# Two transformer-like layers on one core: ten more gate tiles by seven products, the residual stream in DRAM, normalized rows in whole tiles

## The chip, the core and the metric

The kernel runs on one NeuronCore of one Trainium2 chip. The metric is the device time of one execution in microseconds (us). Three executions of the kernel before took 2176.94, 2178.32 and 2180.31 us; the median is 2178.32 us. Times in this document that are stamped like 571.04 are microseconds from the start of the profiled span.

## What is computed

Two layers, each with three sublayers around a residual stream x of 512 tokens by 1024 features. Every sublayer normalizes x, does its work, normalizes the result and adds it to x. In outline, from the reference:

```python
for l in range(DEPTH):                                   # DEPTH = 2
    h = rms_norm(x, gn[0])
    x = x + 0.5 * rms_norm(swiglu(h, w_ffn1_gate[l], w_ffn1_up[l], w_ffn1_down[l]), gn[1])
    h = rms_norm(x, gn[2])
    proj = h @ w_in[l]
    hq, hf, hi, hg, aq, ak, av, gate_a, gate_b = jnp.split(proj, IN_SPLITS, axis=-1)
    y_hg = hgrn2_mixer(hq, hf, hi, hg, lb_all[l], hgrn_head_gain[l]) @ w_branch_hgrn[l]
    y_at = swa_sink_attention(aq, ak, av, attn_sinks[l]) @ w_branch_attn[l]
    mixed = jax.nn.sigmoid(gate_a) * y_hg + jax.nn.sigmoid(gate_b) * y_at
    x = x + rms_norm(mixed @ w_out[l], gn[3])
    h = rms_norm(x, gn[4])
    x = x + 0.5 * rms_norm(swiglu(h, w_ffn2_gate[l], w_ffn2_up[l], w_ffn2_down[l]), gn[5])
```

A swiglu is `(silu(h @ w_gate) * (h @ w_up)) @ w_down` with 2816 hidden features. gate_a and gate_b are 1024 features each: the *branch gates*, 8 tiles of 128 features each, 16 in all per layer.

## The kernel before

**Numbers in two parts.** All large products are in float32 accuracy from fp32r parts: every operand is split into hi (a cast) and lo (the rest), and one block product is three matmuls, hi by hi, hi by lo and lo by hi (mm3, L277 to L279, all recorded at L103). Weights come as tiles of 128 rows by 1024 columns into w32 (4 buffers, loads at L187 on SP's queue). ScalarE (ACT) casts them to whi (L219); wlo comes from VectorE (DVE, L226) or, for kinds v, a and d, from an ACT negation (L223) and an accumulating DMA that GpSimd (POOL) issues (L224). TensorE (PE) holds a 128x128 weight block and streams 512 tokens past it.

**Seven products for eight.** Where a gate tile and an up tile (or any two tiles of 128 features) stand over the same h, the pair is a 2x2 block product, and *fast* computes it with seven products for eight on halves: 256 tokens and half of the contraction. It needs sums of the weights (tt tiles, DVE L206, L207, L212, L213, from the two w32 tiles of the pair; items b and c of the weight stream) and sums of h (tiles x56 and x37, made by *sums* and *quarter_sums*, L340 to L348, one call per two of the eight row tiles of h, and split by L294 on ACT and L295 on DVE), and puts the products together on DVE (L682, L684, L689, L690). In the first FFN 16 of the 22 pairs go that way, in each of the other three 18: 70 in all. The first pairs of each FFN go by plain products (*quad*, *project*, *twice*), which gives DVE time to make the sums.

**The mixer** first makes the projections of the attention and of the recurrence. Then come the branch gates: *branch* makes one tile of gate by *project* (24 matmuls of 512 columns), takes a tanh (ACT L1020), multiplies the attention's or the recurrence's output by a branch weight (12 matmuls) and joins them with one DVE instruction (L1025). Eight calls are for gate_b, eight for gate_a. Beside the gate_b tiles runs the rest of the recurrence, one head after the other, as coroutines that the program steps at points set by a planner's cost table (WAIT): its matmuls stand between those of the gates in the order of PE, which is written out by hand. One step of it: the products p1 and p2 of two blocks of tokens (L828 to L841), their copies from PSUM on ACT as s1 (L835) and s2 (L842), and then, for the same head, the ten products of po (L878; PE L103 aux<-s,s 128x128), of which the fourth already reads s2; then the head's normalization (ACT L881, L884; DVE L883 to L892).

**Residual stream.** x lies in one SBUF tile, x_all, of 128 partitions by 4 by 1024. *lay* fills it at the start of the first FFN: 32 transposes on PE through three PSUM buffers (aux), copied out by ACT and DVE in turn (L401). *post* adds to it in place (L570), *norm* reads it.

**Rows of h.** For the FFNs other than the first, class Halves keeps h in halves of 256 tokens, for the mixer class Pre keeps whole rows of 512.

**Order.** PE's order is fixed by the program. ACT, DVE, POOL and the DMA queues get their instructions in an order that a scheduler settles before the run; `pin` (keep_in_program_order) ties those that are marked to the order of the program among each other. On each engine the instructions then run strictly in that order.

## Time and profile before

| | before |
|---|---|
| the three executions (median) | 2176.94, 2178.32, 2180.31 (2178.32) us |
| the profiled execution: its time, its span | 2179.35 us, 2177.6 us |
| PE busy, DVE busy, ACT busy, POOL busy (share of the span) | 99%, 63%, 48%, 6% |
| mean clock granted to TensorE | 0.998 of full |
| moved by DMA | 262.55 MB, 121 GB/s |

The span runs from the first to the last instruction; 1.75 us of the profiled time lie around it. "PE <- DVE" in a list of waits is idle time of PE that ended when DVE's result came. A row of a timeline gives the start, the duration, engine, line, operation, output and inputs, and in brackets the idle time of the engine ahead of it. Matmuls are pipelined: the duration of one is its latency, and the spacing of the starts tells the rate.

### The profile page before, as it was taken

What the parts mean: (1) busy time and instruction counts of PE and PEld (TensorE: products, weight loads), DVE (VectorE), ACT (ScalarE), POOL (GpSimd) and SP (SyncE); (2) the same over time, 40 slices, a digit from 0 to 9 for tenths busy, and PEclk for the clock granted to TensorE, in tenths of its full rate; (3) what the DMA queues carried; (4) which work ended last, traced back from release to release, by engine and by line L of the source; (5) the groups of instructions that cost most, each with busy time, mean ns of one, the idle gap of its engine ahead of it and who ended that gap; (6) DMA issues with size and microseconds to landing.
All of it is one profiled execution on the core that took longest, in us unless ns stands there. A gap on an engine that the chain in (4) does not pass through costs nothing.

```text
span 2177.6 us, 34576 instructions
## 1 busy us (share of the span) xinstructions
PE 2161.6 (99%) x13625; PEld 1951.4 (90%) x13625; DVE 1369.7 (63%) x2381; ACT 1043.5 (48%) x1703; POOL 124.2 (6%) x148
## 2 busy tenths in 40 slices
PE   9999999999999999999999999999999999999998
PEld 7999988888888999998899998898788889999987
DVE  6887725856734768783487786267566438687823
ACT  6565515354423555562355554254543336565612
POOL 0111000000000011100001110000000000111000
PEclk9999999999999999999999999999999999999999
DMA  7587632211223258773237874322112332578721
GB/s 236 121 185 180 173 97 78 87 59 59 70 95 97 81 130 182 180 203 97 73 107 162 192 184 147 96 86 68 53 64 78 97 97 88 137 179 184 187 89 39
DMA packets 126131, 262.55 MB, mean 121 GB/s; under 512 B 13360, under 2 KB 71184, under 8 KB 125968
## 3 DMA queue, kind: packets, MB, share of 16 engines
q1 hardware_dynamic: 105088, 203.13, 29.7%
q0 software_dynamic: 20736, 57.16, 15.0%
q8 instruction: 107, 1.75, 0.3%
q14 instruction: 56, 0.46, 0.1%
q10 hardware_dynamic: 144, 0.05, 0.0%
HBM read 200.99 MB, written 2.15 MB: 93 GB/s over the span
## 4 chain that ended last, share of the span: by engine, by line
PE 95%; DVE 2%; DMA 1%; ACT 1%; issue 1%; SPq 0%; POOL 0%; DVEq 0%; POOLq 0%; ACTq 0%
PE acc L103 70%; PE aux L103 23%; PE aux L110 1%; DMA w<-wall 1%; PE acc L110 1%; DMA s<-xin 0%; DVE s L453 0%; DMA wlo<-w 0%; DVE s L940 0%; DVE wlo L226 0%; DVE s L771 0%; DMA g_sb<-gains 0%; DVE s L566 0%; ACT s L509 0%; DVE s L576 0%
## 5 line engine op out<-in xcount | busy, mean ns | idle before, releaser
L103 PE MATMUL acc<-s,whi 128*128 128x256 f32 (+1 forms) x5104 | 1096.1, 312 | 1.6 <-ACT whi L219 0.9
L103 PEld LDWEIGHTS acc<-s,whi 128*128 128x128 f32 x5104 | 833.2, 191 | 48.3 <-DVE s L701 1.1
L103 PE MATMUL acc<-s,wlo 128*128 128x256 f32 (+1 forms) x2552 | 791.0, 310 | 0.1
L219 ACT CAST whi<-w 128x1024 fp32r<-128x1024 f32 (+1 forms) x373 | 360.7, 969 | 664.0 <-PE aux L103 270.0
L226 DVE TENSOR_TENSOR wlo<-w,whi 128x1024 fp32r<-128x1024 f32 (+1 forms) x229 | 278.5, 1218 | 405.1 <-ACT whi L219 399.6
L103 PEld LDWEIGHTS acc<-s,wlo 128*128 128x128 f32 x2552 | 487.2, 191 | 26.2 <-DVE wlo L226 0.4
L103 PE MATMUL acc<-whi,s 128*128 128x512 f32 x1296 | 425.2, 393 | 0.0
L103 PEld LDWEIGHTS acc<-whi,s 128*128 128x128 f32 x1296 | 243.9, 188 | 51.3
L103 PE MATMUL acc<-wlo,s 128*128 128x512 f32 x648 | 252.9, 390 | 0.0
L224 POOL DMA_DIRECT2D wlo<-w x144 | 124.0, 861 | 1909.9 <-DVE s L347 689.0
L103 PE MATMUL aux<-whi,s 128*128 128x512 f32 x624 | 207.8, 390 | 0.0
L103 PE MATMUL aux<-s,whi 128*128 128x256 f32 x1120 | 204.6, 283 | 0.0
L226 DVE TENSOR_TENSOR wlo<-tt,whi 128x1024 fp32r<-128x1024 f32 x140 | 170.6, 1218 | 10.1 <-ACT whi L219 9.7
L103 PEld LDWEIGHTS aux<-s,whi 128*128 128x128 f32 x1120 | 174.7, 192 | 0.0
L219 ACT CAST whi<-tt 128x1024 fp32r<-128x1024 f32 x140 | 145.7, 1041 | 26.8 <-PE acc L103 26.3
L103 PE MATMUL aux<-s,wlo 128*128 128x256 f32 x560 | 158.5, 283 | 0.0
L103 PEld LDWEIGHTS acc<-wlo,s 128*128 128x128 f32 x648 | 122.1, 188 | 23.7
L103 PEld LDWEIGHTS aux<-whi,s 128*128 128x128 f32 x624 | 117.1, 188 | 24.1
L206 DVE TENSOR_TENSOR tt<-w,w 128x512 f32<-128x512 f32 x70 | 48.4, 691 | 126.8 <-DMA w<-wall 116.9
L223 ACT ACTIVATE wlo<-w 128x1024 fp32r<-128x1024 f32 (+1 forms) x144 | 122.0, 847 | 0.0
L103 PE MATMUL aux<-wlo,s 128*128 128x512 f32 x312 | 121.4, 389 | 0.0
L103 PEld LDWEIGHTS aux<-s,wlo 128*128 128x128 f32 x560 | 107.5, 192 | 0.0
(164 smaller groups left out, 1888.2 us busy)
## 6 DMA issues: line engine op xcount, KB each, us to landing
w<-wall SPq DMA_DIRECT2D x283, 512.0 KB, 3.5
w<-wall SPq DMA_DIRECT2D x352, 128.0 KB, 2.6
wlo<-w POOLq DMA_DIRECT2D x74, 512.0 KB, 6.0
wlo<-w POOLq DMA_DIRECT2D x70, 256.0 KB, 4.1
grow<-rows_d SPq DMA_DIRECT2D x6, 512.0 KB, 4.9
s<-xin SPq DMA_DIRECT2D x8, 256.0 KB, 6.7
y<-s SPq DMA_DIRECT2D x8, 256.0 KB, 2.5
w<-wall SPq DMA_DIRECT2D x2, 256.0 KB, 4.1
```

Of the source, the lines that this page charges most:

```text
L103: nc.tensor.matmul(o, lhsT, rhs, start=start, stop=stop)
L110: nc.tensor.transpose(o, src, ident)
L206: nc.vector.tensor_tensor(self.t13[:, h[0]], w[:, h[0]], v[:, h[0]], op=ALU.add)
L219: i = nc.scalar.copy(it.hi[:, c], w[:, c])
L223: nc.scalar.mul(it.lo[:, c], w[:, c], -1.0)
L224: nc.gpsimd.dma_start(it.lo[:, c].bitcast(F32), w[:, c], accum_op=ALU.add)
L226: nc.vector.tensor_tensor(it.lo[:, c], w[:, c], it.hi[:, c].bitcast(F32), op=ALU.subtract)
```

## The change

Four things at once.

1. **Branch gates.** Of the 16 tiles per layer, six (the first six of gate_b, `LATE = 6`) stay as they were. The last two of gate_b and the eight of gate_a go in pairs through `sevenths`, the body of the old *fast*: five pairs per layer, seven products for eight, 84 matmuls of 256 columns for 48 of 512. The tanh reads the joined result m (for the second tile of a pair with scale -0.5). The weight stream gets the matching items (`gates`).
2. **Sums one tile ahead.** `sums` now belongs to Pre. In the mixer it is called four times, before the gate_b tiles 2, 3, 4 and 5; in an FFN other than the first twice before the first gates and once before each of the next two. Each call makes, from whole rows, two additions of 512 columns (L450), the four quarter sums (L352 to L355, 256 columns each) and two splits of 512 columns (ACT L302, DVE L303).
3. **Whole rows of h.** Halves goes; the FFNs use Pre. The two plain pairs that went by *twice* (two passes of 256 columns) go by *project* (512 columns).
4. **Residual in DRAM.** x_all goes; 48 pieces of 128x512 are stored to x_d after `lay` (L411) and after each `post` (L558), and loaded again late in each `down` (L523). The pool of large tiles grows from 53 to 61.

Besides, three DVE instructions are now pinned: the first weight sum of each pair (before L206, now L214) and the gating multiplications (before L701 and L707, now L682 and L688). The core of the diff:

```diff
-SLOTS = 53
+SLOTS = 61
-W32, WS, AHEAD, TAIL, PLAIN, FIRST, EARLY = 4, 6, 3, 2, 4, 6, 4
+W32, WS, AHEAD, TAIL, PLAIN, FIRST, EARLY, LATE = 4, 6, 3, 2, 4, 6, 4, 6
...
-    x_all = const([P, TT, D], "x_all")
-    xt = [[x_all[:, t, h * S : (h + 1) * S] for h in range(2)] for t in range(TT)]
+    x_d = dr.tile([TT, 2, P, S], F32, name="x_d")
...
-                nc.vector.tensor_tensor(self.t13[:, h[0]], w[:, h[0]], v[:, h[0]], op=ALU.add)
+                pin(nc.vector.tensor_tensor(self.t13[:, h[0]], w[:, h[0]], v[:, h[0]], op=ALU.add))
...
-                    (nc.vector.tensor_copy if h else nc.scalar.copy)(xt[t][h], p)
+                    x = big()
+                    (nc.vector.tensor_copy if h else nc.scalar.copy)(x, p)
+                    nc.sync.dma_start(x_d[t, h], x)
...
+        def sums(self):
+            k = len(self.x56)
+            a = []
+            for hi, lo in (self.h[k], self.h[k + 4]):
+                f = big()
+                nc.vector.tensor_tensor(f, hi.bitcast(F32), lo.bitcast(F32), op=ALU.add)
+                a.append([f[:, c] for c in HALF])
+            for x, v in zip((self.x56, self.x37), quarter_sums(a[0][0], a[1][0], a[0][1], a[1][1])):
+                x.append(v)
...
         for j in range(kt // 2 - TAIL):
+            if j == kt // 2 - TAIL - 1:
+                for t in range(TT):
+                    for h in range(2):
+                        xt[t][h] = big()
+                        nc.sync.dma_start(xt[t][h], x_d[t, h])
...
                 nc.vector.scalar_tensor_tensor(xt[t][h], yg[h], rc, xt[t][h], op0=ALU.mult, op1=ALU.add)
+                if pre:
+                    nc.sync.dma_start(x_d[t, h], xt[t][h])
...
-                nc.vector.tensor_tensor(z, og, pre.rb, op=ALU.mult)
+                pin(nc.vector.tensor_tensor(z, og, pre.rb, op=ALU.mult))
...
-                if j < 4:
-                    pre.sums()
-                gated(twice(pre), twice(pre))
+                pre.sums()
+                gated(project(pre), project(pre))
...
+        def branches(get):
+            v = sevenths(pre)
+            src = get()
+            for i in range(2):
+                g = big(F32, [P, 2, H2])
+                nc.scalar.activation(out=g, in_=v[:, 2 * i : 2 * i + 2, :], func=AF.Tanh, scale=-0.5 if i else 0.5)
+                p = acc()
+                for k in range(4):
+                    wmm(p, ws.next(), src[k], k == 0, k == 3)
+                g = g.rearrange("p i t -> p (i t)")
+                nc.vector.scalar_tensor_tensor(g, g, 1.0, p, op0=ALU.add, op1=ALU.mult)
+                yield g
...
-        part = [branch(m, attended) for m in range(KT)]
+        part = []
+        for m in range(LATE):
+            if m >= LATE - 4:
+                pre.sums()
+            part.append(branch(attended))
+        part += [g for m in range(LATE, KT, 2) for g in branches(attended)]
         mixed = []
-        for m in range(KT):
-            g = branch(m, recurred)
-            nc.vector.tensor_tensor(g, g, part[m], op=ALU.add)
-            mixed.append(split(g, 0.5))
+        for m in range(0, KT, 2):
+            for g in branches(recurred):
+                nc.vector.tensor_tensor(g, g, part[len(mixed)], op=ALU.add)
+                mixed.append(split(g, 0.5))
```

Lines from here on, in the rows, are those of the kernel that the row belongs to; the changed kernel's lines are other numbers (L842 became L822, L835 became L815, L219 became L227, L226 became L234, L881 became L861, L1025 became L1005, L294 became L302).

**Place one: ACT in the mixer, at head 2 of the recurrence.** First ACT's order before, from the copy of head 2's s1 to the squares of its po; then the same stretch in the changed kernel.

```order
L835 COPY s_5715<-aux_5716 128x256
L219 CAST whi_5896<-w_965_5583 128x1024
L842 COPY s_5738<-aux_5739 128x512
L881 ACTIVATE s_5762<-aux_5751 128x512
L884 ACT_TABLE_LOAD
```

```order
L815 COPY s_5755<-aux_5756 128x256
L227 CAST whi_5974<-w_981_5623 128x1024
L302 CAST s_5785<-s_5779 128x512
L302 CAST s_5789<-s_5780 128x512
L822 COPY s_5797<-aux_5798 128x512
L861 ACTIVATE s_5821<-aux_5810 128x512
L864 ACT_TABLE_LOAD
```

Two casts of the first call of `sums` now stand ahead of the copy of s2 (L842, now L822). They read s_5779 and s_5780, which DVE makes in the next piece. At head 3 two casts of the second call stand ahead of its copy of s2 in the same way, and both places come again in layer 1.

**The same place on DVE.** The changed kernel's order from the end of gate_b tile 1 (L1005); before, the first row was followed at once by the 128x4 product, the wlo of the weights and the reduction (L883, now L863).

```order
L1005 SCALAR_TENSOR_TENSOR s_5726<-s_5726,acc_5728 128x512
L450 TENSOR_TENSOR s_5775<-s_3760,s_3761 128x512
L450 TENSOR_TENSOR s_5777<-s_3786,s_3787 128x512
L767 TENSOR_TENSOR s_5610<-s_5610 128x4
L234 TENSOR_TENSOR wlo_5975<-w_981_5623,whi_5974 128x1024
L352 TENSOR_TENSOR s_5779<-s_5777,s_5775 128x256
L355 TENSOR_TENSOR s_5780<-s_5775 128x256
L353 SCALAR_TENSOR_TENSOR s_5779<-s_5779,s_5775 128x256
L215 TENSOR_TENSOR tt_6071<-w_1003_5771 128x512
L354 SCALAR_TENSOR_TENSOR s_5780<-s_5779,s_5777 128x256
```

Two additions of 512 columns, a weight split of 1024, four of 256 columns and one more of 512 now stand between the end of the gate tile and the second cast on ACT.

**Place two: DVE at the start of the first FFN.** The names: L701 to L704 before, L682 to L685 now, are the multiplications of the plain gates 0 to 2; L206 and L207 before, L215 now, are weight sums for the first fast pair; L401 is a copy of `lay`. First the order before, then now, from the first gate's first multiplication.

```order
L701 TENSOR_TENSOR s_386<-acc_210,s_374 128x512
L703 TENSOR_TENSOR s_387<-acc_211,s_374 128x512
L701 TENSOR_TENSOR s_392<-acc_212,s_374 128x512
L703 TENSOR_TENSOR s_393<-acc_213,s_374 128x512
L701 TENSOR_TENSOR s_453<-acc_340,s_374 128x512
L704 TENSOR_TENSOR s_387<-s_387,s_386 128x512
L704 TENSOR_TENSOR s_393<-s_393,s_392 128x512
L1092 TENSOR_SCALAR hgh<-hgh 128x256
L1095 TENSOR_TENSOR lbmx<-lb_in 128x4
L206 TENSOR_TENSOR tt_683<-w_74_384,w_82_445 128x512
```

```order
L682 TENSOR_TENSOR s_386<-acc_210,s_374 128x512
L684 TENSOR_TENSOR s_387<-acc_211,s_374 128x512
L215 TENSOR_TENSOR tt_699<-w_82_445 128x512
L685 TENSOR_TENSOR s_387<-s_387,s_386 128x512
L682 TENSOR_TENSOR s_392<-acc_212,s_374 128x512
L684 TENSOR_TENSOR s_393<-acc_213,s_374 128x512
L685 TENSOR_TENSOR s_393<-s_393,s_392 128x512
L1093 TENSOR_SCALAR hgh<-hgh 128x256
L1096 TENSOR_TENSOR lbmx<-lb_in 128x4
```

A weight sum that reads the same load, w_82, has moved from behind the gates' multiplications to the third row. Gate 2's multiplications and the copies of `lay` on DVE stand behind all of these.

**The same place on ACT**, the changed kernel's order from gate 0's silu on. L683 is a silu, L227 and L231 are weight casts and negations, L1099 is the exp of the lower bounds, L410 a copy of `lay`. Before, the three silus stood together ahead of the exp (L702 and L1098), and behind the exp came the first copy (L401), a weight cast, two copies, a weight negation and the last copy.

```order
L683 ACTIVATE s_386<-s_386 128x512
L231 ACTIVATE wlo_573<-w_62_308 128x1024
L683 ACTIVATE s_392<-s_392 128x512
L227 CAST whi_604<-w_65_338 128x1024
L1099 ACT_TABLE_LOAD
L1099 ACTIVATE lbex<-lbex 128x8
L410 COPY s_452<-aux_447 128x512
L231 ACTIVATE wlo_605<-w_65_338 128x1024
L683 ACT_TABLE_LOAD
L683 ACTIVATE s_455<-s_455 128x512
L410 COPY s_474<-aux_469 128x512
```

The silu of gate 2 now stands behind the exp with a table load of its own, and three of ACT's four copies of `lay` stand behind it.

More of the change, by code (lines that the diff above doesn't have):

```diff
@@ L160, in pairs, with gates @@
                 self.n += 2
+        def gates(self):
+            u, h = self.n, (slice(0, D // 2), slice(D // 2, D))
+            self.src[u + 1] = [(h[0], wall[u + 1][:, h[1]]), (h[1], wall[u + 2][:, h[0]])]
+            self.src[u + 2] = [(h[0], wall[u + 1][:, h[0]]), (h[1], wall[u + 2][:, h[1]])]
+            self.pairs(1)
+            self.plain(1)
         def rows(self, kt):
@@ L421, in raw @@
         def raw(self, half, i):
-            return [x[half + i] for x in self.x124]
-    class Pre:
+            return [[x[half + i][:, j, :] for j in range(2)] for x in self.x124]
+    class Pre(Quarters):
         def __init__(self, l, n):
@@ L432, in __init__, with raw @@
             self.xn = {}
+            self.x56, self.x37 = [], []
+        def sums(self):
[7 more added lines that the diff above has]
+                x.append(v)
+        def raw(self, half, i):
+            return [cut(self.h[k + 4 * i], HALF[half]) for k in range(4)]
         def turn(self, half, get):
@@ L603, in down @@
         return pre
-    def of_half(pre, k, half):
-        h = pre.h[k]
-        if isinstance(pre, Halves):
-            return [h[half][:, i, :] for i in range(2)]
-        return h if half is None else cut(h, HALF[half])
     def quad(pre, halves):
@@ L622, in quad @@
                         blocks[k, j] = ws.next(uses=2 if halves else 1)
-                    wmm(o[j][:, c], blocks[k, j], of_half(pre, k, half), k == 0, k == KT - 1)
+                    wmm(o[j][:, c], blocks[k, j], cut(pre.h[k], c), k == 0, k == KT - 1)
             ws.pinned = False
-        return o
-    def twice(pre):
-        o = acc()
-        blocks = [ws.next(uses=2) for _ in range(KT)]
-        for half in (0, 1):
-            for k in range(KT):
-                wmm(o[:, HALF[half]], blocks[k], of_half(pre, k, half), k == 0, k == KT - 1)
         return o
@@ L1047, in trunk @@
             if n == 2:
-                ws.plain((4 * H + 4 + 2 + 2 * KT) * KT // 8 + 2 * KT * 4 // 8)
+                ws.plain(2 * H + 6 + 8 + LATE * 3 // 2)
+                for _ in range(KT - LATE // 2):
+                    ws.gates()
                 ws.rows(KT)
```

109 lines of the change are left out of this document (39 added, 70 removed).

## The prediction

> **What bounds the kernel now.** I read the page first, for the busy shares and the chain that ended last; then the list of what PE waits for; then timelines of PE, ACT and DVE where the change moves instructions.
>
> ```profile
> span 2177.6 us, 34576 instructions
> ...
> PE 2161.6 (99%) x13625; PEld 1951.4 (90%) x13625; DVE 1369.7 (63%) x2381; ACT 1043.5 (48%) x1703; POOL 124.2 (6%) x148
> ...
> PE 95%; DVE 2%; DMA 1%; ACT 1%; issue 1%; SPq 0%; POOL 0%; DVEq 0%; POOLq 0%; ACTq 0%
> ```
>
> PE is busy 99% of the span and holds 95% of the chain. So work taken from PE shortens the run by its whole length, and every wait that PE is given lengthens it by its whole length, however idle the other engines are on average.
>
> ```profile
> PE acc L110 <- DVE x_all L570: 2.5, 1, 2.5
> PE aux L103 <- DVE s L295: 1.5, 2, 0.7
> ...
> PE aux L110 <- DVE x_all L401: 0.7, 1, 0.7
> ```
>
> These are sums of PE's waits, how often, and the longest, costliest first. Apart from the end (2.5 us) no group is over 1.5. There is almost nothing to win from waits, and much room for new ones.
>
> **PE's saving.** Rates are read from the spacing of starts, not from durations. The four rows are two stretches, of 512 columns and of 256; each row is two of the three matmuls of a group.
>
> ```profile
> 627.98 0.61 PE L103 MATMUL acc<-s,whi 128*128 128x512 f32 x2
> 631.38 0.62 PE L103 MATMUL acc<-s,whi 128*128 128x512 f32 x2
> 739.97 0.40 PE L103 MATMUL acc<-s,whi 128*128 128x256 f32 x2
> 745.37 0.40 PE L103 MATMUL acc<-s,whi 128*128 128x256 f32 x2
> ```
>
> From 627.98 to 631.38 lie five groups, 15 matmuls: 3.40 / 15 = 226.7 ns each. From 739.97 to 745.37 lie 15 groups, 45 matmuls: 120.0 ns. A narrow matmul costs 6.7 ns more than half a wide one, so seven products for eight save less than an eighth.
>
> Gates: 10 pairs, each 84 x 120.0 = 10.08 us for 48 x 226.7 = 10.88: 10 x -0.80 = -8.0 us. Plain FFN pairs by whole rows: two pairs, that is four projections, in each of three FFNs, 12 x (24 x 226.7 - 48 x 120.0 ns) = 12 x -0.32 = -3.8 us. Together **-11.8 us**. TensorE: Matmul & The Clock Gate of the Trainium skill (section "Wait — 56ns, not 53.3ns?") gives columns / 2.4 GHz + 2.5 ns, that is 215.8 and 109.2 ns here, by which the two parts would be -11.9 and -0.7; this trace has neither figure (226.7 and 120.0 ns), and its rows decide.
>
> **What is added in the mixer.** The rows are ACT, PE and DVE at head 2 of the recurrence, and below them head 3.
>
> ```profile
> 570.56 0.58 ACT L842 COPY s<-aux 128x512 f32<-128x512 f32 x1 [1.16 <-PE aux L103]
> ...
> 571.04 2.39 PE L103 MATMUL aux<-s,s 128*128 128x128 f32 x20
> ...
> 569.19 0.68 DVE L1025 SCALAR_TENSOR_TENSOR s<-s,acc 128x512 f32<-128x512 f32 x1
> 569.79 0.15 DVE L787 TENSOR_TENSOR s<-s 128x4 f32<-128x4 f32 x1
> 569.86 1.21 DVE L226 TENSOR_TENSOR wlo<-w,whi 128x1024 fp32r<-128x1024 f32 x1
> ...
> 583.64 0.68 DVE L295 TENSOR_TENSOR s<-aux,s 128x512 fp32r<-128x512 f32 x1
> 584.24 0.28 DVE L833 TENSOR_SCALAR s<-s,s 128x128 f32<-128x128 f32 x1
> ...
> 586.00 0.59 ACT L842 COPY s<-aux 128x512 f32<-128x512 f32 x1 [2.13 <-PE aux L103]
> ...
> 586.50 2.17 PE L103 MATMUL aux<-s,s 128*128 128x128 f32 x18
> ```
>
> PE begins po at 571.04, and its fourth product, some 0.3 us on, reads what L842 has copied by 571.14. ACT had waited 1.16 us for that copy's input, so the copy runs as soon as it can. After the change two casts stand ahead of it, and their inputs are late. From the rows: 512 columns on DVE take 0.68 us and follow one another at 0.60 (569.19 to 569.79, 583.64 to 584.24); 256 columns and casts:
>
> ```profile
> L345 DVE SCALAR_TENSOR_TENSOR s<-s,s 128x256 f32<-128x256 f32 x16 | 6.7, 418 | 0.0
> ...
> L294 ACT CAST s<-s 128x512 fp32r<-128x512 f32 x120 | 67.6, 617 | 20.7 <-DVE s L345 19.6 <-DVE s L346 0.9
> ```
>
> With the same overlap of 0.08, 256 columns follow at 0.34. DVE from 569.79: two additions 1.20, the small product 0.07, the weight split 1.14, three quarter sums 1.02: 573.2. A weight sum 0.60 and the last quarter sum 0.42: 574.2. ACT's second cast runs from there to 574.8 and the copy to 575.4. PE wanted it at 571.36: **4.0 us** of PE idle. Nothing hides it, since PE's order is fixed and its next matmul is the one that waits.
>
> At head 3, the second call: DVE has the additions from 584.6 to 585.8 (ahead of them now stand all four small scalings, of which two came behind the split before), three quarter sums to 586.8, the last to 587.2; the casts follow from 586.9 and end by 588.0, the copy by 588.6, against 586.59 before: **2.0 us**. The third and fourth call have no PE work behind them that is due soon: 0. Both layers have the place: 2 x 6.0 = **+12.0 us**.
>
> The pairs themselves add DVE and ACT work where there is room: in the gates' stretch DVE was 17.73 us busy of 50 (first row), and in the FFNs the same body runs at 39.89 of 50 (second).
>
> ```profile
> 600.00:650.00 50.00, 17.73 (x19) 1.00 0.30 96
> 850.00:900.00 50.00, 39.89 (x57) 1.00 0.82 185
> ```
>
> **What is added at the start.** First FFN, layer 0, where `lay` copies x out of PSUM:
>
> ```profile
> 42.30 0.69 DVE L206 TENSOR_TENSOR tt<-w,w 128x512 f32<-128x512 f32 x1 [0.98 <-DMA w<-wall]
> 44.92 0.68 DVE L401 COPY x_all<-aux 128x512 f32<-128x512 f32 x1
> ...
> 41.62 1.28 ACT L1098 ACT_TABLE_LOAD   x1
> 43.71 0.59 ACT L401 COPY x_all<-aux 128x512 f32<-128x512 f32 x1 [0.34 <-PE aux L110]
> ...
> 43.08 1.93 PE L110 MATMUL aux<-ident,s 128*128 128x128 f32 x16
> 45.66 1.09 PE L110 MATMUL aux<-ident,s 128*128 128x128 f32 x8 [0.65 <-DVE x_all L401]
> 46.99 1.09 PE L110 MATMUL aux<-ident,s 128*128 128x128 f32 x8 [0.24 <-ACT x_all L401]
> 47.84 0.71 PE L103 MATMUL acc<-s,whi 128*128 128x512 f32 x2
> ```
>
> The weight sum waited for its load until 42.30, which cost nothing since the gates' multiplications were done. Now it is DVE's third row and the load is no earlier, so from 38.0 to 42.3 DVE stands, with the multiplications behind it. Then four rows of 512 bring ACT its second silu at 44.2; the cast, a table load (1.28) and the exp put ACT's first copy of `lay` at 47.3 instead of 43.71, and DVE's, behind the exp's small rows and two multiplications, at 49.3 instead of 44.92. The third copy waits for ACT's weight negation, another table load and a silu, until 50.7. PE has three buffers, so the eight groups of four transposes end at 52.6 instead of 47.84: **+4.8 us**. Where the first copy were on time, this falls to about 0.
>
> **What a wait costs beyond itself.** The last wait of PE, ahead of 2171.39, shows that the granted clock (the column after the busy times) follows idleness:
>
> ```profile
> 2168.00:2171.00 3.00, 0.94 (x5) 1.00 0.62 175
> 2171.00:2171.50 0.50, 0.11 (x1) 1.00 0.00 0
> 2171.50:2172.00 0.50, 0.50 (x4) 0.50 0.00 0
> ...
> 1.50:4.00 2.50, 2.50 (x14) 1.00 0.80 231
> 4.50:6.00 1.50, 1.50 (x15) 1.00 0.88 270
> ```
>
> After 2.45 us without work it is 0.50. How long work takes to bring it back is bounded by the start: there PE does 14 small matmuls in 2.5 us, and from about 4 us on 15 in 1.5, so nearly 3 us of work go at 1/1.78 of the rate (the column reads 1.00 there, the counts do not). That is 2.9 x (1 - 1/1.78) = 1.3 us lost. The bounds are 0 and twice that. The waits of 4.0, 4.0 and 4.8 us are all longer than 2.45; I take 1.3 for each, **+3.9 us**, and none for those of 2.0. The same page of the Trainium skill, section "What's actually happening", says that the clock is set by free-running windows of 3.4 us. The drop in this trace, 2.5 us after the last work, fits a window that was mostly idle. By that rule a wait of 4 us may fall across two windows and cool nothing, and one of 2 us could never fill one.
>
> **At nothing.** Stores and loads of x (256 KB each, SP): post's last piece of a `down` is ready, and the next weight load stands behind its store.
>
> ```profile
> 367.77 1.42 DVE L570 SCALAR_TENSOR_TENSOR x_all<-s,rt,x_all 128x512 f32<-128x512 f32 x2
> ...
> 372.54 1.46 SPq L187 DMA_DIRECT2D w<-wall  x2
> ...
> w<-wall SPq DMA_DIRECT2D x2, 256.0 KB, 4.1
> ```
>
> At 369.19 the last store can go, and the load is issued at 372.54, when its buffer comes free: 3.3 us of cover for two issues of 0.73. If the cover is gone, the gates start up to 1.5 us later in each of five places. The loads of x stand ahead of weight loads in `down`; what they wait for has no row, so 0 to one landing of their size (4.1 us) in each of six; I take 0, as the stores' row has it, and keep the rest for the upper end. The FFNs' sums keep their place beside the plain pairs (PE's 1.3 us shorter stretch there is inside their lead): 0, at worst 1.3 in each of three.
>
> **The sum.** 2179.35 - 11.8 + 12.0 + 4.8 + 3.9 = 2188.3 for a profiled run; that run lay 1.0 over the median, so **2187 us**, 0.4% slower. 0.2%, 4.4 us, is about what a measurement of this kernel can tell from no change.
>
> **Rivals.**
> - *All hidden* (the side of faster): head 2's copy decides. If DVE reached the first addition 4 us earlier than 569.79, at about 565.8, and ACT stood free at the start, only the saving would be left: 2178.3 - 11.8 = 2166.5. Against it: DVE ends the gate tile's row at 569.79, and the order puts the additions behind that row. Chance 0.12.
> - *Waits in the mixer alone*, the start hidden or the load earlier: 2178.3 - 11.8 + 12.0 + 2.6 = 2181; without cooling 2178.5. The same. Chance 0.15.
> - *Waits without cooling* (the windows of the rule fall well): 2178.3 + 5.0 = 2183.3, just slower. Chance 0.17.
> - *DVE's weight sums ahead of the joins.* In each fast pair of the FFNs the first weight sum stands now right ahead of the next pair's first join. Before, it waited 1.67 us per pair for a load:
>
> ```profile
> DVE tt L206 <- DMA w<-wall: 116.9, 50, 4.9
> ```
>
>   116.9 / 70. DVE has 10.08 - 8.0 = 2.1 us free in a pair and now also waits 0.7 for the silu. If the load comes as late as before, each pair slips by 0.3 us: 70 x 0.3 = 20, 2207 us. For it: the place. Against: that load is of a buffer that comes free a pair earlier. Chance 0.12.
>
> The forecast (2185 to 2191) has 0.44. The range leaves out most of *all hidden* and the far end of the last rival: **2174 to 2204**. Faster 0.12; same 0.16 (the second rival and the edge of the third); slower 0.72.
>
> **What would show it.** Right: PE aux L103 waits near 4 and 2 us for ACT L822 in both layers; PE L110 waits in sum near 5 us for L410; the clock at 0.5 for some 3 us behind each of the long ones; PE's rates at 226.7 and 120.0 ns. Wrong: no wait at L822 (all hidden), DVE's L215 waiting for loads in the FFNs with PE waiting behind it (the last rival), or PE waiting for whi or wlo in the branch pairs, which I have at nothing.

## The result, and the profile after

The changed kernel took 2187.57 us, the median of five executions (2184.43 to 2188.43). The kernel before took 2178.32 on the same chip (2176.76 to 2180.31). The ratio is 1.004, with a 95% interval of 1.0025 to 1.0055: slower by 0.4%, where 2187 us was predicted. The execution that was profiled is the slowest of the five, 2188.43.

The page of the changed kernel, its lines on the span, the engines, the chain that ended last, and the new stores (KB each, then median us from issue to landing):

```profile
span 2186.4 us, 35185 instructions
...
PE 2156.7 (99%) x13697; PEld 1952.8 (89%) x13697; DVE 1462.5 (67%) x2501; ACT 1104.1 (51%) x1769; POOL 141.4 (6%) x168
...
PE 94%; DVE 4%; ACT 1%; issue 0%; DVEq 0%; ACTq 0%
...
x_d<-s SPq DMA_DIRECT2D x48, 256.0 KB, 2.0
```

PE is busy 4.9 us less and the span is 8.8 us longer: PE's lead is spent on waits and, as the windows below show, on a lower clock. What PE waits for in the changed kernel (sum, times, longest):

```profile
PE aux L103 <- ACT s L822: 10.6, 4, 3.5
PE aux L110 <- ACT s L410: 3.1, 1, 3.1
PE acc L110 <- DVE s L556: 2.5, 1, 2.5
PE aux L110 <- DVE s L410: 2.0, 1, 2.0
PE aux L103 <- DVE s L303: 1.5, 2, 0.7
```

The third and fifth were there before (as L570 and L295). New are the first, the second and the fourth: the mixer's 10.6 us, and 5.1 us at the start, where the kernel before waited 0.9 (L401).

Where the two programs stand in time is read from the starts of the same matmul of PE at the ends of the stages. The last column is what each stretch alone added:

| stretch of PE, up to | before | after | added |
|---|---|---|---|
| end of the first plain gates (start of layer 0) | 50.71 | 57.11 | +6.40 |
| end of the first FFN | 372.66 | 379.06 | 0.00 |
| mixer of layer 0, up to the gate pairs | 597.27 | 609.26 | +5.59 |
| the five gate pairs | 693.25 | 701.35 | -3.89 |
| out-projection | 747.52 | 755.81 | +0.19 |
| plain pairs of the second FFN | 967.92 | 974.95 | -1.26 |
| its end | 1098.38 | 1105.60 | +0.19 |
| layer 1: plain pairs of the first FFN | 1318.77 | 1324.73 | -1.26 |
| its end | 1449.42 | 1455.39 | +0.01 |
| mixer, up to the gate pairs | 1675.69 | 1689.96 | +8.30 |
| the five gate pairs | 1771.70 | 1782.07 | -3.90 |
| out-projection | 1825.97 | 1836.54 | +0.20 |
| plain pairs of the second FFN | 2046.37 | 2055.68 | -1.26 |
| end of the span | 2177.6 | 2186.4 | -0.51 |

The sum is +8.8. The saving is -11.57, and three places give back +20.3.

**The saving.** A stretch of a gate pair on PE:

```profile
659.76 0.40 PE L103 MATMUL acc<-s,whi 128*128 128x256 f32 x2
...
664.44 0.40 PE L103 MATMUL aux<-s,whi 128*128 128x256 f32 x2
```

From 659.76 to 664.44 lie 13 groups of three: 4.68 / 39 = 120.0 ns each, the spacing that the FFNs' pairs had before. Nothing in the pairs waits.

**The mixer.** Head 2 of layer 0 on DVE:

```profile
576.21 1.28 DVE L450 TENSOR_TENSOR s<-s,s 128x512 f32<-128x512 f32 x2
577.49 1.22 DVE L234 TENSOR_TENSOR wlo<-w,whi 128x1024 fp32r<-128x1024 f32 x1
...
580.24 0.41 DVE L354 SCALAR_TENSOR_TENSOR s<-s,s 128x256 f32<-128x256 f32 x1
```

On ACT:

```profile
579.75 0.62 ACT L302 CAST s<-s 128x512 fp32r<-128x512 f32 x1 [3.92 <-DVE s L353]
580.68 0.62 ACT L302 CAST s<-s 128x512 fp32r<-128x512 f32 x1 [0.32 <-DVE s L354]
581.21 0.58 ACT L822 COPY s<-aux 128x512 f32<-128x512 f32 x1
```

On PE, here and at the same step of layer 1: the products that wait, and as the last row of each the same weight product, 28 matmuls on.

```profile
577.48 0.83 PE L103 MATMUL aux<-s,s 128*128 128x128 f32 x6
...
581.84 1.83 PE L103 MATMUL aux<-s,s 128*128 128x128 f32 x14 [3.53 <-ACT s L822]
...
586.06 0.76 PE L103 MATMUL acc<-s,whi 128*128 128x512 f32 x2
```

```profile
1659.78 3.35 PE L103 MATMUL aux<-s,s 128*128 128x128 f32 x14 [3.54 <-ACT s L822]
...
1666.76 0.53 PE L103 MATMUL acc<-s,whi 128*128 128x512 f32 x1
```

ACT stands for 3.92 us with its first cast, whose input DVE makes behind the two additions and the weight split. The copy L822 has had its input since about 577 (in E1 below, where no cast is in its way, it waits 1.16 us for it), but its place is behind both casts. PE waits 3.53 us in layer 0 and 3.54 in layer 1. The wait is the same; what follows it is not. From its end to that weight product PE takes 586.06 - 581.84 = 4.22 us in layer 0 and 1666.76 - 1659.78 = 6.98 in layer 1, for the same work. Windows of PE (busy time, granted clock, then the share and rate of DMA), cut where the clock changed and in layer 0 at the same distance, say why:

```profile
576.84:580.25 3.41, 1.47 (x10) 1.00 0.14 22
580.25:583.66 3.41, 1.82 (x15) 1.00 0.34 132
...
1655.45:1658.86 3.41, 0.79 (x7) 1.00 0.29 88
1658.87:1662.28 3.41, 2.50 (x11) 0.50 0.18 72
1662.28:1665.69 3.41, 3.41 (x11) 0.50 0.00 0
1665.70:1669.10 3.40, 3.40 (x19) 1.00 0.00 0
```

In layer 0 the clock stayed at 1.00 through the wait. In layer 1 it fell to 0.50 before the wait was over and stayed there for nearly 6 us of work. That is 2.76 us on top of the wait, and the difference of the two mixers, 8.30 - 5.59 = 2.71.

The trace also suggests why one wait cooled the clock and the other did not. The stretch at half clock is 6.83 us long, and so is the one at the start, shown next; the two begin 1611.1 us apart (47.77 and 1658.87), which is 472 times 3.413, half of 6.827. So the clock changes here at points of a fixed grid. Cut by that grid, layer 1's wait has 2.6 us of its 3.5 in one window, and layer 0's is divided into 1.9 and 1.6. How much idleness it takes is not settled: both kernels also have one stretch of 3.41 us at 0.50 in layer 1's mixer (from 1563.29, on the same grid; before the change from 1557.11), behind a window in which PE was idle for only 1.06 us.

**The start.** DVE at the start of the first FFN, from the first gate's second multiplication on:

```profile
37.30 0.68 DVE L684 TENSOR_TENSOR s<-acc,s 128x512 f32<-128x512 f32 x1
42.03 0.69 DVE L215 TENSOR_TENSOR tt<-w 128x512 f32<-128x512 f32 x1 [4.04 <-DMA w<-wall]
...
49.82 1.28 DVE L410 COPY s<-aux 128x512 f32<-128x512 f32 x2
```

And PE there:

```profile
43.02 1.47 PE L110 MATMUL aux<-ident,s 128*128 128x128 f32 x12
47.57 0.96 PE L110 MATMUL aux<-ident,s 128*128 128x128 f32 x4 [3.08 <-ACT s L410]
50.56 3.68 PE L110 MATMUL aux<-ident,s 128*128 128x128 f32 x16 [2.03 <-DVE s L410]
53.89 1.04 PE L103 MATMUL acc<-s,whi 128*128 128x512 f32 x2
```

DVE stands 4.04 us for the weights of L215, its first copy of `lay` starts at 49.82 instead of 44.92, and PE has filled its three buffers by 44.5. Its two waits are 5.1 us, 4.2 more than before. The last 16 transposes take 3.33 us (50.56 to 53.89), and the windows there show the clock at half from 47.77 to 54.60:

```profile
44.36:47.77 3.41, 0.33 (x4) 1.00 0.48 135
47.77:51.18 3.41, 1.38 (x7) 0.50 0.64 184
51.18:54.60 3.42, 3.42 (x17) 0.50 1.02 290
```

So of the 6.4 us lost here 4.2 are waits and 2.2 are clock: about 1.6 in those transposes, half of 3.33, and the rest in the four transposes ahead of them and the first matmuls behind (53.89 to 57.11 is 3.22 us, for the 2.87 from 47.84 to 50.71 before).

### The profile page after: what moved, and what is told of

It is laid out like the page before. It is cut to its first block, busy times and chain, and to the rows that moved or that the text cites. A ratio compares the mean times of both kernels' runs of the same rounds, so it can differ in the third digit from the quotient of the medians.

```text
span 2186.4 us, 35185 instructions
## 1 busy us (share of the span) xinstructions
PE 2156.7 (99%) x13697; PEld 1952.8 (89%) x13697; DVE 1462.5 (67%) x2501; ACT 1104.1 (51%) x1769; POOL 141.4 (6%) x168
## 4 chain that ended last, share of the span: by engine, by line
PE 94%; DVE 4%; ACT 1%; issue 0%; DVEq 0%; ACTq 0%
PE acc L103 68%; PE aux L103 24%; PE aux L110 2%; DVE s L477 1%; DVE wlo L234 0%; PE acc L110 0%; DVE s L564 0%; ACT s L489 0%; DVE s L552 0%; ACT whi L227 0%; DVE s L920 0%; ACT s L302 0%; DVE s L450 0%; DVE s L556 0%; DVE s L751 0%
## 5 line engine op out<-in xcount | busy, mean ns | idle before, releaser
L103 PE MATMUL acc<-s,whi 128*128 128x256 f32 (+1 forms) x4992 | 1061.4, 310 | 0.7 <-DVE s L682 0.7
L103 PEld LDWEIGHTS acc<-s,whi 128*128 128x128 f32 x4992 | 812.3, 191 | 42.3 <-DVE s L682 1.1
L103 PE MATMUL acc<-s,wlo 128*128 128x256 f32 (+1 forms) x2496 | 768.8, 308 | 0.0
L227 ACT CAST whi<-w 128x1024 fp32r<-128x1024 f32 (+1 forms) x373 | 355.9, 956 | 579.2 <-PE aux L103 275.6
L234 DVE TENSOR_TENSOR wlo<-w,whi 128x1024 fp32r<-128x1024 f32 (+1 forms) x209 | 254.0, 1217 | 349.0 <-ACT whi L227 343.2
L103 PE MATMUL aux<-s,whi 128*128 128x256 f32 x1280 | 233.8, 283 | 0.0
L227 ACT CAST whi<-tt 128x1024 fp32r<-128x1024 f32 x160 | 167.8, 1049 | 122.0 <-DVE tt L214 67.5
L234 DVE TENSOR_TENSOR wlo<-tt,whi 128x1024 fp32r<-128x1024 f32 x160 | 195.5, 1222 | 24.3 <-ACT whi L227 21.6
L103 PEld LDWEIGHTS aux<-s,whi 128*128 128x128 f32 x1280 | 199.7, 192 | 0.0
L103 PE MATMUL aux<-s,wlo 128*128 128x256 f32 x640 | 181.1, 283 | 0.0
L231 ACT ACTIVATE wlo<-w 128x1024 fp32r<-128x1024 f32 (+1 forms) x164 | 138.6, 845 | 0.0
L103 PEld LDWEIGHTS aux<-s,s 128*128 128x128 f32 (+1 forms) x768 | 87.9, 192 | 24.7 <-ACT s L822 11.4
```

The lines of the kernel that those rows point to most:

```text
L103: nc.tensor.matmul(o, lhsT, rhs, start=start, stop=stop)
L227: i = nc.scalar.copy(it.hi[:, c], w[:, c])
L231: nc.scalar.mul(it.lo[:, c], w[:, c], -1.0)
L234: nc.vector.tensor_tensor(it.lo[:, c], w[:, c], it.hi[:, c].bitcast(F32), op=ALU.subtract)
```

## The experiments

All are timed against the kernel before on the same chip: 2177.98 us (E1 to E4), 2178.26 (E5 to E8), 2178.66 (E9 to E11). The first theory was that of the prediction: the time is lost where an instruction that PE needs stands behind others on ACT or DVE that are not due, so moving those gives the time back. The rivals were that another wait stands behind the one removed, and that a cooled clock, and not the order, makes up most of the loss.

**E1: the mixer's sums two tiles later.** The four calls of *sums* go into the last two plain gate tiles, two in each, instead of one in each of the last four.

```diff
-            if m >= LATE - 4:
+            if m >= LATE - 2:
+                pre.sums()
                 pre.sums()
```

> The changed kernel with one edit: the four calls of sums in the mixer come before gate_b tiles 4 and 5, two at each, for one at each of the tiles 2 to 5. Their casts then stand behind head 3's copy of s2 on ACT. Theory (the casts hold the copies of s2, PE waits for them, and the longest wait cools the clock): PE's waits for L822, 10.6 us in four places, go, and with them the stretch at half clock behind the wait of layer 1; by the stages of the two traces the mixers lose 5.6 and 8.3 us, so 2187.6 - 13.9 = 2173.7, or up to 2 more in each layer if the sums are now late for the first branch pair. Rival (the five pairs' own work on ACT, DVE and the weight queue is too much, the place of the sums does not matter): the mixers stay as long, 2186 to 2188. Second rival (the traffic of x_d): no change either.

Measured: 2176.41 us (2175.04 to 2177.94), ratio 0.9993 (0.9985 to 1.0002): 11.2 us less than the changed kernel. ACT's copy at head 2 now:

```profile
577.61 0.59 ACT L822 COPY s<-aux 128x512 f32<-128x512 f32 x1 [1.16 <-PE aux L103]
```

It waits 1.16 us for its own input, just as before the change, and the waits at L822 are gone. But PE's list has a new one:

```profile
PE acc L103 <- DVE s L303: 2.2, 2, 1.1
```

It is the splitting of the sums (L303) in the first gate pair, which takes 11.92 us instead of 10.07: 1.85 lost per layer. E1's expectation had allowed up to 2 us in each layer for this, beside its figure of 2173.7; the run came out 2.7 us above that figure. The mechanism in the mixer is shown; its cure costs a part of what it gives.

**E2: L215 of the first pair pinned,** so that it cannot stand ahead of the gates' multiplications.

```diff
-                nc.vector.tensor_tensor(self.t13[:, h[1]], v[:, h[0]], v[:, h[1]], op=ALU.add)
+                i = nc.vector.tensor_tensor(self.t13[:, h[1]], v[:, h[0]], v[:, h[1]], op=ALU.add)
+                if u == 2 * FIRST:
+                    pin(i)
```

> The changed kernel with one edit: the second half of the weight sum of the first fast pair (L215, the third row of DVE's order in the first FFN) is pinned too, which puts it behind the first half, some fifty rows later. The stores of lay to x_d stay. Theory (DVE stands from 38.0 to 42.3 behind that row's load, and the copies of lay come late for it): the 6.4 us that the start loses shrink to about 1.3, since ACT's table load and the silu of gate 2 still stand ahead of three copies; no wait there is long enough to cool the clock. 2187.6 - 5.1 = 2182.5. Rival (the eight stores of lay hold SP's queue, or PSUM buffers come free late for the stores' sake): the start stays 6.4 us longer than before, 2187.6.

Measured: 2187.02 us (2186.14 to 2188.17), ratio 1.0044 (1.003 to 1.0058). That is 0.55 us less than the changed kernel, which the spread of the runs does not tell from nothing. In E2's trace L215 is out of the way, and the first plain gates end at 55.30, 1.8 us sooner than in the changed kernel but still 4.6 late; layer 0's mixer, which had kept its clock there, is at half clock from 581.34 to 584.75 in this execution and gives 1.6 of the 1.8 back. DVE's first copy of `lay` (L412 here) still starts 3.57 us later than before the change:

```profile
47.29 0.68 DVE L684 TENSOR_TENSOR s<-acc,s 128x512 f32<-128x512 f32 x1
...
48.49 1.28 DVE L412 COPY s<-aux 128x512 f32<-128x512 f32 x2
```

Ahead of it stand gate 2's multiplications, which come behind a row of small instructions on the lower bounds, and those waited 2.82 us for ACT's exp. So the wait for a load at L215, which the prediction named, is one delay of several in a row, and with it gone the next one holds.

**E3: E1 and E2 together.**

> The edits of the first two runs together. Theory: the two are far apart in time and add up: 2187.6 - 13.9 - 5.1 = 2168.6, 10 us under the kernel before, close to what PE's saving alone gives (2178.3 - 11.6 = 2166.7). Rivals: if the saving is not there, no better than before, 2178; if the traffic of x_d costs several us, 2172 to 2175.

Measured: 2175.47 us (2174.39 to 2177.01), ratio 0.9988 (0.9979 to 0.9997). That is E1 less 0.9 us; the start still ends 5.7 us late. It missed for the same reason as E2.

**E4: the mixer of the kernel before** in the changed kernel: no gate pairs and no sums there.

```diff
-        for m in range(LATE):
-            if m >= LATE - 4:
-                pre.sums()
-            part.append(branch(attended))
-        part += [g for m in range(LATE, KT, 2) for g in branches(attended)]
+        part = [branch(attended) for m in range(KT)]
...
-        for m in range(0, KT, 2):
-            for g in branches(recurred):
+        for m in range(KT):
+            g = branch(recurred)
```

> The changed kernel with the mixer of before: all 16 branch gates by plain products, no sums in the mixer; whole rows of h, x in DRAM and the pins stay. Theory: it gives back the gates' saving (7.8 us by the two traces) and is rid of the mixers' loss (13.9 us), the start keeps its 6.4 us: 2187.6 + 7.8 - 13.9 = 2181.5. Rival (the loss in the mixers is the traffic of x_d or the whole rows, not the sums): 2187.6 + 7.8 = 2195.

Measured: 2180.24 us (2179.49 to 2180.99), ratio 1.0011 (1.0002 to 1.002). It gives up 7.8 us of saving and is still 7.3 us below the changed kernel, so the mixers' loss in the changed kernel is about 15.1 us in the median; E1 gives 14.9 (11.2, and 2 x 1.85 of new wait). No wait at L822 is left; those at the start are.

**E5: four tiles of their own for the copies of `lay`,** and the first gates unpinned, on top of E3. The thought was that the copies take tiles of the shared pool that gate 2 wants.

```diff
-SLOTS = 61
+SLOTS = 57
...
-                    x = big()
+                    x = sb.tile([P, S], F32, tag="xl", name=nm("xl"), bufs=4)
...
-                pin(nc.vector.tensor_tensor(z, og, pre.rb, op=ALU.mult))
+                nc.vector.tensor_tensor(z, og, pre.rb, op=ALU.mult)
```

> The third run's kernel (sums late, the weight sum's second half pinned) with two more edits at the start of the first FFN: the copies of lay go to four tiles of their own, out of the pool that the gates' results come from (61 tiles become 57 and 4), and the gates' multiplications of the first FFN are not pinned. In the order of DVE and ACT all that stood between the gates and the copies of lay is then as in the kernel before. Theory (the start's loss is the order on DVE and ACT, from the pin and from the shared pool together): the 5.7 us that the third run still loses at the start go, PE waits under 1 us there and the clock stays at full: 2175.5 - 5.5 = 2170. Rival (the stores of lay themselves, on SP ahead of the next weight loads, hold the start): it still loses about 5 us, 2175.

Measured: 2176.55 us (2175.28 to 2178.95), ratio 0.9992 (0.9983 to 1.0001). A miss. The order came out like that before, but four tiles for eight copies make the last four wait for the stores of the first four, here one of ACT's two that do:

```profile
55.09 0.59 ACT L412 COPY xl<-aux 128x512 f32<-128x512 f32 x1 [3.38 <-DMA x_d<-xl]
```

The start ends as late as in the changed kernel. This tells nothing for or against the order; it shows that the stores are free only where no tile waits for one.

**E6: only the residual in DRAM** added to the kernel before (copies, stores and loads as in the changed kernel, 61 tiles).

```diff
-    x_all = const([P, TT, D], "x_all")
-    xt = [[x_all[:, t, h * S : (h + 1) * S] for h in range(2)] for t in range(TT)]
+    x_d = dr.tile([TT, 2, P, S], F32, name="x_d")
...
-                    (nc.vector.tensor_copy if h else nc.scalar.copy)(xt[t][h], p)
+                    x = big()
+                    (nc.vector.tensor_copy if h else nc.scalar.copy)(x, p)
+                    nc.sync.dma_start(x_d[t, h], x)
```

> The kernel before with one part of the change: the residual stream in DRAM (copies of lay to tiles of the pool of 61, 48 stores, 48 loads), no pins, the FFNs and the mixer as before. Theory (the traffic itself is hidden; the pool puts gate 2's multiplications and so DVE's copies of lay behind the weight sums that wait for their load until 42.3): the start loses 2.8 us, or 4.3 if the clock cools there, all else stays within 1 us: 2181 to 2183. Rival (traffic costs in each of the six sublayers, 1 us or more): 2187 and more. Rival (the pins alone made the loss at the start): 2178.

**E7: only the three pins** added to the kernel before (the first is the weight sum, the others the gating).

```diff
-                nc.vector.tensor_tensor(self.t13[:, h[0]], w[:, h[0]], v[:, h[0]], op=ALU.add)
+                pin(nc.vector.tensor_tensor(self.t13[:, h[0]], w[:, h[0]], v[:, h[0]], op=ALU.add))
...
-                nc.vector.tensor_tensor(z, og, pre.rb, op=ALU.mult)
+                pin(nc.vector.tensor_tensor(z, og, pre.rb, op=ALU.mult))
...
-                nc.vector.tensor_tensor(u, ou, z, op=ALU.mult)
+                pin(nc.vector.tensor_tensor(u, ou, z, op=ALU.mult))
```

> The kernel before with one part of the change: the three pins, nothing else; x stays in SBUF. DVE then has the second half of the first weight sum as its third row, as in the changed kernel, but no wait for tiles of the pool. Theory (that row holds DVE until 42.3, and ACT's silus come late for it): the start loses about 2.7 us, or 4.2 if the clock cools: 2181 to 2182.5. Rival (the loss at the start comes from the residual in DRAM alone): 2178.

Measured: E6 2181.62 us (2180.42 to 2184.49), ratio 1.0017 (1.0008 to 1.0026); E7 2180.78 us (2180.06 to 2184.17), ratio 1.0014 (1.0005 to 1.0023). In the traces E6's first gates end 5.53 us late, E7's 3.64. PE's waits there, first in E6:

```profile
PE aux L110 <- ACT s L401: 2.0, 1, 2.0
PE aux L110 <- DVE s L401: 1.9, 1, 1.9
```

and in E7:

```profile
PE aux L110 <- DVE x_all L401: 3.0, 2, 2.7
```

Each part alone breaks the start, and both together cost 6.4, not 9.2. In E7 the second half of the weight sum (L207), which has no pin, is DVE's third row and waits 4.74 us for its load, as L215 does in the changed kernel; and gate 2's first multiplication, now tied to the order of the pinned small rows on the lower bounds, comes at 51.92 behind them, for 39.16 before. In E6 the copies take tiles of the shared pool; no pin is needed there for a weight sum to get ahead of the multiplications:

```profile
43.05 0.69 DVE L205 TENSOR_TENSOR tt<-w,w 128x512 f32<-128x512 f32 x1 [3.57 <-DMA w<-wall]
...
48.57 0.66 DVE L401 COPY s<-aux 128x512 f32<-128x512 f32 x1
```

That the tiles of the pool bring this about is argued here from the order alone; E9 tests it.

**E8: PE kept busy.** In the changed kernel, 16 additional matmuls of ones by ones before head 2's first product that needs s2; they compute nothing that is used.

```diff
+                    if t == 2 and i == 2:
+                        for _ in range(16):
+                            nc.tensor.matmul(po[:, 3 * P :], ones, ones, start=True, stop=True)
```

> The changed kernel with 16 idle matmuls (ones by ones, into a part of po that is overwritten after them) put on PE ahead of head 2's first product of s2, in both layers: PE works through most of the 3.5 us for which it waits there. They add work and change no result. Theory (a wait cools the clock, in some executions and at half rate for two windows of 3.4 us, and that costs up to 3 us beside the wait): the clock stays at full in both mixers, the waits for L822 shrink to some 0.3 us but the stretch stays as long, and the time is the lowest that the changed kernel had, 2184.5 instead of 2187.6. Rival (the clock's fall costs nothing, since PE waits for others there): no change, 2187.6, or longer by what the idle matmuls overrun.

Measured: 2185.33 us (2184.04 to 2186.14), ratio 1.0031 (1.002 to 1.0043). The idle work takes 3.74 us, so its end (581.60) is where the wait ended before (581.84); only the clock differs, at both places now:

```profile
580.00:584.00 4.00, 4.00 (x33) 1.00 0.31 120
...
1658.00:1662.00 4.00, 4.00 (x33) 1.00 0.30 119
```

The medians differ by 2.2 us; the intervals of the two ratios overlap, so this alone doesn't settle the size of the cooling. That the cooling comes from PE's idleness, and goes with it, the windows of this one execution show; its grid lies within half a microsecond of the changed kernel's (its other stretches at half clock begin at 47.30 and 1562.82, for 47.77 and 1563.29).

**E9: sums late, and gate 2 ahead of `lay`.** E1's sums; the planner's cost *lay* in the table WAIT at 34000 for 32000, so that gate 2's multiplications claim their tiles of the pool first; and the first FFN's gates without their pin. The order on PE stays the same but for one row.

```diff
-    early=0.0, first=0.0, spread=2750.0, squares=1700.0, lay=32000.0, laid=1500.0, normed=6300.0, final=2600.0,
+    early=0.0, first=0.0, spread=2750.0, squares=1700.0, lay=34000.0, laid=1500.0, normed=6300.0, final=2600.0,
...
-                pin(nc.vector.tensor_tensor(z, og, pre.rb, op=ALU.mult))
+                nc.vector.tensor_tensor(z, og, pre.rb, op=ALU.mult)
...
-            if m >= LATE - 4:
+            if m >= LATE - 2:
+                pre.sums()
                 pre.sums()
```

> The changed kernel with the sums late (as in the first run) and two edits at the start of the first FFN: the coroutine lay begins a little later in the program (34000 for 32000 in the cost table), so that gate 2's multiplications claim their tiles of the pool ahead of lay's copies while PE's order stays, but for one row; and the first FFN's gates are not pinned. Lay's copies stay in the pool of 61, so none waits for a store; the weight sum's second half stays unpinned. In the order, DVE and ACT have gates, silus and copies as before the change. Theory (what the start loses is order alone: tiles claimed by lay ahead of gate 2, and the pin): the start loses at most 0.5 us, its clock stays at full, 2176.4 - 6 = 2170.4. Rival (the stores of lay hold something that no order cures): it still loses 4 to 6, 2175.

Measured: **2169.99 us** (2169.59 to 2171.79), ratio 0.9962 (0.995 to 0.9975): faster than both, by 8.7 us than the kernel before on its chip and by 17.6 than the changed one. PE at the start:

```profile
45.77 1.53 PE L110 MATMUL aux<-ident,s 128*128 128x128 f32 x12 [0.49 <-DVE s L410]
47.49 0.66 PE L110 MATMUL aux<-ident,s 128*128 128x128 f32 x4 [0.20 <-ACT s L410]
47.91 0.71 PE L103 MATMUL acc<-s,whi 128*128 128x512 f32 x2
```

The last row stood at 47.84 before the change and at 53.89 after it. The copies still take tiles of the pool and the eight stores are still there, so what the start had lost is order: which tiles are claimed first, and the pin. The clock is 1.00 here and in both mixers (three windows):

```profile
40.00:60.00 20.00, 19.31 (x102) 1.00 0.82 230
564.00:584.00 20.00, 19.82 (x112) 1.00 0.16 53
1640.00:1670.00 30.00, 29.82 (x166) 1.00 0.16 43
```

**E10: E9 with three calls of *sums* in the fifth tile and one in the sixth,** against the wait in the first gate pair.

```diff
-                pre.sums()
+                for _ in range(3 if m == LATE - 2 else 1):
+                    pre.sums()
```

> The kernel of the run before with three calls of sums ahead of gate_b tile 4 and one ahead of tile 5, for two and two. In the first run PE waited 1.1 us in each layer for the last split of the sums (L303) in the first branch pair. Theory (the sums only have to come a little sooner there): those waits shrink to under 0.3, 2.0 us less than the run before, 2168.4, which is what PE's saving alone gives within 2 us (2178.3 - 11.6 = 2166.7). Rival (DVE is full between the tiles 4 and the first pair, and what comes sooner delays the weight sums by as much): no gain, 2170.4.

Measured: 2170.11 us (2169.4 to 2172.69), ratio 0.9965 (0.9952 to 0.9979): as E9. The wait for L303 went, and another took its place:

```profile
PE aux L103 <- DMA wlo<-w: 2.3, 2, 2.0
```

**E11: only the start of E9,** with the mixer as changed (the edits of E9 to `lay` and the pin).

> The changed kernel with the two edits at the start alone (lay later in the program, the first FFN's gates not pinned); the sums of the mixer stay where the change put them. Theory: the start's 6.4 us go, the mixers' 13.9 stay: 2187.6 - 6.2 = 2181.4. Rival (the two losses are linked, as in one clock state that is carried on): the mixers lose more or less than before.

Measured: 2181.66 us (2178.7 to 2184.46), ratio 1.0017 (1.0009 to 1.0026). The eleven times fall into groups: one of 2178.70 at a mean clock of 0.998, six from 2180.60 to 2182.81 (0.996 to 0.998), four from 2183.82 to 2184.46 (0.995). Only the first has a trace; in it the mixers' waits are those of the changed kernel, 10.6 us. The clock stays at 1.00 through layer 1's long wait, which the grid divides into 1.9 and 1.6 us, and falls once, to 0.50 from 576.36 to 579.77, behind layer 0's, of which 2.15 us lie in one window. So with the same program and the same waits the cooling comes in the one layer or in the other. That the other two groups have one and two more such places, some 2.8 us each, fits layer 1 of the changed kernel, but is inferred from the times and the clocks.

E1, E9, E11 and the changed kernel make a square (medians in us):

| | sums as changed | sums late |
|---|---|---|
| start as changed | 2187.57 | 2176.41 |
| start restored | 2181.66 | 2169.99 |

The mixer's sums are worth 11.2 and 11.7, the start 5.9 and 6.4: the two losses add up. The four were timed in three sessions, in which the kernel before lay at 2178.32, 2177.98 and 2178.66, so each step is uncertain by some 0.5 us.

## Why the prediction came out right

- **What bounds it, and the saving: right.** PE's rate and the saving are as worked out: gates -7.79 for -8.0, plain pairs -3.78 for -3.8.
- **The mixer's waits: right in mechanism, a little large.** DVE's additions, then the casts, then the copy, in that order on ACT: 3.53 and about 1.78 us per layer for 4.0 and 2.0, 10.6 in all for 12.0. E1 and E4 show that the sums cause it.
- **The clock: the mechanism is right, the term mis-sized, the evenness wrong.** 1.3 us per long wait was taken, 2.6 the upper bound. Where it happened in a mixer it cost 2.76, above both; in layer 0 it didn't happen. The bound assumed that about 3 us of work bring the clock back; in layer 1 it was at 0.50 from 1658.87 to 1665.69, 6.8 us, of which 5.9 were work. The Trainium skill, page TensorE: Matmul & The Clock Gate, section "What's actually happening", speaks of free-running windows of 3.4 us. The traces agree: in every one the stretches at 0.50 ahead of the program's end are 3.41 or 6.83 us long, and where a trace has several, they begin a whole number of 3.413 us apart. What the prediction drew from it, that a wait of 2 us could never fill a window, does not mean that such a wait cools nothing: in E6 the clock fell to 0.50 at 47.38, behind one wait of 1.95 us (44.79 to 46.74). In the profiled run the three places gave 0, 2.8 and 2.2 us, 5.0 in sum for the 3.9 predicted.
- **The start: the size is near, the reason is only partly right.** 4.8 of waits was predicted and 4.2 found, 1.3 of clock and 2.2 found: 6.4 us in all for 6.1. But "where the first copy were on time, this falls to about 0" put the loss on DVE's first copy, and that on L215's wait for its load. E2 removed that wait, and its start still lost 4.6 of the 6.4 us. E6 and E7 show two causes, each enough: copies that take tiles of the shared pool, and the pins. E9 and E11 undo both and bring the start back.
- **The sum: close in part by luck.** The span grew by 8.8 us where 8.9 was added up, but the waits were 14.8 us for 16.8, the clock 5.0 for 3.9, the saving 11.6 for 11.8, and 0.6 of small changes had no term. The errors offset each other.
- **At nothing.** Stores and loads of x: +0.2 us in three places, by the table, so the cover held. The FFNs' sums: 0.00 and 0.01. PE waiting for its own sums or weight parts in the gate pairs did not show in the changed kernel; it shows in E1 (1.85 us per layer) and E10, once the sums are later.
- **The rivals.** *All hidden* would be 2166.5; E9 comes to 2170.0 when the order is mended, and the rest of 3.5 is about what the first gate pair of each layer loses (2 x 1.85). *Waits in the mixer alone* had 2181; E11, with the start mended, is that case and comes to 2181.66. *DVE's weight sums ahead of the joins* did not come:

```profile
DVE tt L215 <- DMA w<-wall: 42.2, 40, 4.4
```

  It is a third of the 116.9 us before, so the loads come early enough, and the first FFN of layer 0 took the same time to 0.01 us.

What stays open: which of the pin and the pool holds what share when both are there, since they overlap, and why E2's exp still comes late, which was read from its order and not tried by itself.

## What to carry to other kernels

Where one engine is busy 99% of the span, a saving on it is safe only as far as the small instructions that feed it keep their places: list for each engine in between what now stands ahead of the copy that the busy engine waits for. Here moving the sums of h by two tiles and giving one gate its tiles before eight copies took 0.4% slower to 0.4% faster, with the same work on PE. When a wait is mended, look for the next one in line before counting the gain, for three cures here (E2, E5, E10) mostly uncovered it.

## What the runs showed of the hardware that was not expected

A wait of PE of 3.5 us cooled the clock in one layer and not in the other, in one execution of one program (1.00 at 582 us, 0.50 at 1660 us), and the time to full clock was 6.8 us where the prediction had 2.9. The two waits lie differently on a grid of 3.41 us, with 2.6 us in one window or 1.9 and 1.6 in two, and E11 fits that too. How much idleness it takes stays open: a window with 1.95 us of it was followed by half clock in E6 and not in layer 0 here, and one with only 1.06 us was, in layer 1's mixer, before and after the change. The program of E11, which has the two long waits in the mixers, spreads over 5.8 us in eleven executions; the kernel before over 3.8 in fifteen on the same chip. The stores of 256 KB, 2.0 us in the median from issue to landing over the changed kernel's 48, took 4.5 in the median for the eight at the start in E5, and held copies there for more than 3 us.
